# A two-layer streaming encoder step on one core: the FFN's second product as a seven-product 2x2x2 block scheme, with operand sums kept in DRAM

## The chip, the core and the metric

The kernel runs on one NeuronCore of a Trainium2 chip. Five engines work side by side, each on its own in-order instruction list: TensorE (PE; matrix products into the accumulation memory PSUM, with its weight loads shown apart as PEld), VectorE (DVE), ScalarE (ACT), GpSimd (POOL) and SyncE (SP), which here does nothing but issue transfers. Sixteen DMA engines move data between DRAM and the on-chip memory SBUF (128 partitions). The metric is the device time of one execution in microseconds (us): median 2997.3 over three runs, from 2995.75 to 2997.85.

## What is computed

One step of an encoder with two layers, on 1024 new "prompt" frames and 64 "sample" frames, handled together as 1088 tokens (`T`) of width 1024 (`D`). Layer 0 is a state-space mixer (SSD) with an FFN behind it, layer 1 a banded attention with an FFN; every part is normalised before and after. The part that matters here:

```python
def swiglu(u, w_in, w_out):
    g, up = jnp.split(u @ w_in, 2, axis=-1)
    return (jax.nn.silu(g) * up) @ w_out
...
xp = xp + rmsnorm(swiglu(rmsnorm(xp, nw[2]), ffn_w_in[layer], ffn_w_out[layer]), nw[3])
```

`w_in` is 1024 x 5632, `w_out` 2816 x 1024. The hidden matrix between the two products has 2816 rows = 22 blocks of 128 (`FT`), for 1088 tokens. The second product, hidden times `w_out`, is what is changed. Everything is float32; each operand is split into a rounded high part and a rest (`h`, `l`), and one 128 x 128 block of a product costs three matmuls: high by high, high by rest, rest by high.

## The kernel before

**Layout and order.** Activations lie transposed: features on the partitions, tokens along the columns. `SL` cuts the tokens into three slices of 384, 384 and 320 columns, `QS` into four quarters of 256, 256, 288 and 288. The order of PE is written by hand: a clock `st.t` in the source advances with each matmul put down, and side tasks (generators: norms, loads, attention steps) are resumed when their due time on that clock has come, so PE's list is fixed when the kernel is built. The other engines' lists are ordered by a scheduler with priorities (`tc.high_priority`; `HIP` is 3000, `LDP` 1500).

**Weights.** Class `Weights` loads each weight tile by SP into a `raw` buffer (two, plus up to `lent.cap` borrowed from the ring `rx`), splits it with one ACT copy and one DVE subtraction (L338, L339) into one of three `hl` buffers, and hands it to PE. `pair` (L288 to L307) forms the sums of weight blocks for the first product on POOL and DVE.

**First product of the FFN.** It already uses the seven-product scheme of 2x2x2 blocks (`run_pair`, one call per hidden block `t_`): the token halves are `b=0` (quarters 0 and 1, 256 wide) and `b=1` (quarters 2 and 3, 288 wide). Six blocks (`NB0`) are first done plainly for `b=0` (`plain_pairs`), while `b=1` is still being prepared; then 16 blocks for both halves, about 21 us each, then the six once more for `b=1` alone, about 11 us each. Each finished hidden tile goes to DRAM (`hscr`): POOL multiplies gate by value (L1293, L1297), SP writes (L1294, L1298).

**Second product.** `loader` fetches `hscr` slice by slice into staging tiles `sg`, and ACT and DVE split them into `rx` and `r` tiles (L1326 to L1328). For each slice `s`, each of 8 output blocks `m` and each of 22 hidden blocks `k`, PE does three matmuls (L1463 to L1465):

```python
PE.matmul(ps[:, :n], wh, xh, start=(k == 0), stop=False)
PE.matmul(ps[:, :n], wh, xl, start=False, stop=False)
PE.matmul(ps[:, :n], wl, xh, start=False, stop=(k == FT - 1))
```

That is 1584 matmuls in each layer. ACT copies each finished PSUM tile to `y` (L1478) and squares it, POOL adds the squares (L477). When a slice is done its `end` task runs: `rb_steps` has PE transpose the sums of squares (`nst`, L484), DVE make the inverse root in nine or ten small steps (L495 to L508), PE spread it again (`nbp`, L514); DVE then scales `y`, adds the residual and SP writes it out. In layer 0 `end` goes on to split `y` for the attention's projections (L1398, L1399), forms a second norm `rb_out` and marks the slice in `done2`. In layer 1 the last slice's `end` is the tail of the kernel: it takes the last tile's squares straight from PSUM (L1474), sums them by a matmul with ones (L489), and lets PE do part of the residual additions (L1357, L1368).

**Attention.** After layer 0, PE projects V, K and Q of the first head pair, slice after slice (L451 to L453). Each Q's low part is copied to the other partition half by a small SBUF transfer (`Ql`, L1604) before the scores (L1676, L1677) use it.

Of the kernel before, what the change touches and what calls it, by code (L numbers as in the profile page):

```python
# [16 lines left out]
P = 128  # L17
# [16 lines left out]
FT = 22  # L34
AH = 16
# [13 lines left out]
EP_W, ER_W, EQ_W = (9.4, 9.4, 2.2), (8.9, 8.9, 3.3), (11.0, 11.0)  # L49
# [4 lines left out]
LDP, ENP, ATP = 1500, (0, 0, 1500), 1000  # L54
# [18 lines left out]
MMR = 2360.0  # L73

# [148 lines left out]
class Weights:  # L223
# [118 lines left out]
    def scaled(self, it, r):  # L342

        self.used.append(self.hl)
        t = self.hl.get()
        for k in range(KD):
            sl, c = slice(k * P, (k + 1) * P), it["kscale"][:, k:k + 1]
            self.nc.scalar.activation(t[:, 0, sl], r[:, sl], AF.Copy, scale=c)
        for k in range(KD):
            sl, c = slice(k * P, (k + 1) * P), it["kscale"][:, k:k + 1]  # L350
            self.nc.vector.scalar_tensor_tensor(t[:, 1, sl], r[:, sl], c, t[:, 0, sl], op0=ALU.mult, op1=ALU.subtract)  # L351
        it["w"] = t[:, 0, :], t[:, 1, :]
# [20 lines left out]
def hybrid_kernel(  # L373
# [36 lines left out]
    hd_ = [dr.tile([P, FT, T], F32, name=f"hscr{i}") for i in range(2)]  # L410
# [32 lines left out]
    def passes(ps, w, rhs, ks, n, parts=2, first=True, last=True):  # L443
# [4 lines left out]
        for i, (kw, k) in enumerate(ks):  # L448
# [4 lines left out]
            PE.matmul(ps[:, :n], l_, xh, start=False, stop=(last and i == nk - 1))  # L453
# [11 lines left out]
    def ssum_start(n):  # L465
        t = nsb.tile([P, 384], F32, tag="ssum", bufs=3, name="ssum")
        if n % P:
            G.memset(t[:, n:], 0.0)
        return t
# [100 lines left out]
    for b in range(2):  # L570
        for half in range(2):
            W.plan(*[dict(src=[w_so[m][:, half * 1024:(half + 1) * 1024]]) for mg in MGS for m in mg])

# [61 lines left out]
    with ExitStack() as es:  # L635
# [426 lines left out]
        finish(2)  # L1062
        for grp in order:
# [147 lines left out]

    def ffn_plan(layer):
        w1, w2 = w_f1[layer], w_f2[layer]
        W.plan(*[dict(src=[w1[i]], acc=t_ < NACC) for t_ in range(NB0) for i in (t_, FT + t_)])
        for t_ in [*range(NB0, FT), *range(NB0)]:
            W.plan(dict(src=[w1[t_], w1[FT + t_]]))
        for s in range(NSL):
            for m in range(KD):
                for k0, nk in KCH:
                    W.plan(dict(src=[w2[m][:, k0 * P:(k0 + nk) * P]], n=nk * P))  # L1220

    KCH = ((0, 8), (8, 8), (16, 6))

    def plain_pairs(ts, ops, hd, px, tmp):
# [3 lines left out]
        for q in range(2):  # L1228
            st.wait_for(lambda: all(a_ in ops.plain for a_ in (f"a{q + 1}1", f"a{q + 1}2")))
            uq = ops.plain[f"a{q + 1}1"] + ops.plain[f"a{q + 1}2"]  # L1230
            for t_, w2 in zip(ts, ws):
                x = tmp.tile([P, n], F32, tag=("p1", "u3")[q] + f"{t_ % 2}", name="x")
# [5 lines left out]
                def mult(ps):  # L1238
                    with tc.high_priority(HIP):
                        V.tensor_tensor(x, ps[:, :n], x, op=ALU.mult)  # L1240
                    nc.sync.dma_start(hd[:, t_, q * n:(q + 1) * n], x)
# [744 lines left out]
```

## Time and profile before

| | |
|---|---|
| median of the runs | 2997.3 us |
| the profiled execution, its time | 2997.29 us |
| its span, first to last instruction | 2995.6 us |
| time around the span | 1.7 us |
| mean granted TensorE clock | 0.994 |
| PE matmuls | 2948.2 us busy, 98% of the span |
| DVE, ACT, POOL | 2044.8, 1460.1 and 699.0 us busy |
| SP's transfer queue | 325.45 MB, 34.3% of sixteen engines' span |

The busy time of PE is a union: matmuls overlap, each lasts about 0.3 us and a new one starts every 0.12 to 0.17 us, so a stage's length is read from the distance between starts. Columns of the stage table: length, busy time (and count) of PE, PEld, DVE, ACT and POOL, the granted clock, the DMA engines' share and rate.

### The profile page before, as it was taken

The page shows a single profiled execution, that of the slowest core. Times are in us where ns is not written, and L with a number is a line of the kernel's source. Part 1 is how long each engine was busy: PE and PEld are TensorE (multiplying, and loading weights), DVE is VectorE, ACT ScalarE, POOL GpSimd, SP SyncE. Part 2 cuts the span into 40 slices and gives each one's busy share as a digit, 9 for nine tenths or more (in the row PEclk, how much of TensorE's full clock was granted, in tenths as well). Part 3 has the DMA queues.
Part 4 walks back from the last instruction along what each step waited for, and adds up shares of the span by engine and source line. Part 5 has one row for each costly group of instructions (what it writes and reads, how often), then busy time and mean ns, then how long its engine had stood idle before and what let it go on. Part 6 is the DMA issues. An engine that isn't in the chain of part 4 may idle for free.

```text
span 2995.6 us, 56513 instructions
## 1 busy us (share of the span) xinstructions
PE 2948.2 (98%) x21722; PEld 2891.8 (97%) x21722; DVE 2044.8 (68%) x4512; ACT 1460.1 (49%) x2643; POOL 699.0 (23%) x848
## 2 busy tenths in 40 slices
PE   8999999999999999999999999999999999999999
PEld 7999999999999999999999899999899999999999
DVE  7778887885768554574557778777778655475544
ACT  6756566564453232244445566555654322244443
POOL 1333333330121433351111000000131343451111
PEclk9999999999999999999999999999999999999999
DMA  3011111124654222255655222222356222245654
GB/s 122 33 59 51 61 50 49 61 68 145 192 150 141 83 73 80 76 161 173 202 177 169 87 76 79 70 65 86 116 171 188 80 76 77 80 148 176 214 179 136
DMA packets 180671, 335.43 MB, mean 112 GB/s; under 512 B 18192, under 2 KB 128400, under 8 KB 180400
## 3 DMA queue, kind: packets, MB, share of 16 engines
q1 hardware_dynamic: 178608, 325.45, 34.3%
q0 software_dynamic: 1792, 6.36, 1.1%
q8 instruction: 171, 2.80, 0.4%
q14 instruction: 100, 0.82, 0.1%
HBM read 264.69 MB, written 62.60 MB: 109 GB/s over the span
## 4 chain that ended last, share of the span: by engine, by line
PE 88%; DVE 7%; DMA 2%; ACT 2%; issue 1%; POOL 0%; SPq 0%; DVEq 0%; ACTq 0%; POOLq 0%
PE px L1264 9%; PE px L1265 9%; PE px L1266 9%; PE mm L451 8%; PE mm L453 8%; PE mm L452 8%; PE po L1464 6%; PE po L1465 6%; PE po L1463 6%; PE mmx L452 3%; PE mmx L451 3%; PE mmx L453 3%; PE po L1747 2%; PE ptp L1708 1%; PE yp L889 1%
## 5 line engine op out<-in xcount | busy, mean ns | idle before, releaser
L451 PE MATMUL mm<-r,hl 128*128 128x384 f32 (+2 forms) x1664 | 554.3, 333 | 6.4 <-DVE dt L698 3.4
L453 PE MATMUL mm<-r,hl 128*128 128x384 f32 (+2 forms) x1664 | 539.9, 324 | 3.2 <-DVE hl L351 2.6
L452 PE MATMUL mm<-r,hl 128*128 128x384 f32 (+2 forms) x1664 | 539.0, 324 | 0.0
L339 DVE TENSOR_TENSOR hl<-raw,hl 128x1024 fp32r<-128x1024 f32 (+1 forms) x219 | 260.6, 1191 | 219.9 <-ACT hl L338 217.3
L1265 PE MATMUL px<-r,hl 128*128 128x288 f32 (+1 forms) x1184 | 348.0, 294 | 0.0
L451 PEld LDWEIGHTS mm<-r,hl 128*128 128x128 f32 x1664 | 315.9, 190 | 9.0 <-ACT BT L775 3.7
L453 PEld LDWEIGHTS mm<-r,hl 128*128 128x128 f32 x1664 | 314.8, 189 | 4.6 <-DVE hl L351 3.7
L452 PEld LDWEIGHTS mm<-r,hl 128*128 128x128 f32 x1664 | 316.1, 190 | 0.0
L1264 PE MATMUL px<-r,hl 128*128 128x288 f32 x1056 | 311.3, 295 | 0.1
L1266 PE MATMUL px<-r,hl 128*128 128x288 f32 x1056 | 311.1, 295 | 0.0
L338 ACT CAST hl<-raw 128x1024 fp32r<-128x1024 f32 (+1 forms) x219 | 219.0, 1006 | 179.9 <-PE po L1465 97.1
L477 POOL TENSOR_TENSOR ssum<-ssum,sq 128x256 f32<-128x256 f32 (+3 forms) x97 | 128.4, 1324 | 640.6 <-ACT sq L476 625.3
L1265 PEld LDWEIGHTS px<-r,hl 128*128 128x128 f32 x1184 | 222.7, 188 | 0.0
L1266 PE MATMUL px<-rx,hl 128*128 128x256 f32 x768 | 216.5, 282 | 4.9 <-DVE hl L339 4.9
L1264 PE MATMUL px<-rx,hl 128*128 128x256 f32 x768 | 217.0, 283 | 0.6 <-ACT hl L338 0.6
L1464 PE MATMUL po<-rx,hl 128*128 128x384 f32 (+1 forms) x624 | 201.7, 323 | 0.1
L1264 PEld LDWEIGHTS px<-r,hl 128*128 128x128 f32 x1056 | 198.7, 188 | 0.5 <-DVE u L1279 0.5
L1266 PEld LDWEIGHTS px<-r,hl 128*128 128x128 f32 x1056 | 198.5, 188 | 0.0
L1463 PE MATMUL po<-rx,hl 128*128 128x384 f32 (+1 forms) x608 | 197.6, 325 | 0.0
L1465 PE MATMUL po<-rx,hl 128*128 128x384 f32 (+1 forms) x608 | 196.7, 323 | 0.0
L1265 PE MATMUL px<-rx,hl 128*128 128x256 f32 x640 | 180.1, 281 | 0.0
L288 POOL TENSOR_TENSOR tt<-raw 128x512 f32<-128x512 f32 x40 | 53.7, 1343 | 439.3 <-DMA raw<-in_w_f_dram 382.8
(367 smaller groups left out, 8163.3 us busy)
## 6 DMA issues: line engine op xcount, KB each, us to landing
raw<-in_w_f_dram SPq DMA_DIRECT2D x154, 512.0 KB, 3.8
rx<-in_w_f_dram SPq DMA_DIRECT2D x54, 512.0 KB, 3.6
raw<-in_w_in_dram SPq DMA_DIRECT2D x40, 512.0 KB, 3.5
sg<-hscr SPq DMA_DIRECT2D x88, 192.0 KB, 3.6
raw<-in_w_f_dram SPq DMA_DIRECT2D x44, 384.0 KB, 3.2
raw<-in_w_so_dram SPq DMA_DIRECT2D x32, 512.0 KB, 3.7
raw<-in_w_kv_dram SPq DMA_DIRECT2D x18, 512.0 KB, 3.5
raw<-in_w_o_dram SPq DMA_DIRECT2D x16, 512.0 KB, 3.6
```

The source lines that it names most:

```text
L338: self.nc.scalar.copy(h, v)
L339: (eng or self.eng or self.nc.vector).tensor_tensor(lo, v, h, op=ALU.subtract)
L451: PE.matmul(ps[:, :n], h_, xh, start=(first and i == 0), stop=False)
L452: PE.matmul(ps[:, :n], h_, xl, start=False, stop=False)
L453: PE.matmul(ps[:, :n], l_, xh, start=False, stop=(last and i == nk - 1))
L477: (eng or G).tensor_tensor(ssum[:, :n], ssum[:, :n], q[:, :n], op=ALU.add)
L1264: PE.matmul(ps, wh, ah[:, k, :], start=(k == 0), stop=False)
L1265: PE.matmul(ps, wh, al[:, k, :], start=False, stop=False)
L1266: PE.matmul(ps, wl, ah[:, k, :], start=False, stop=(k == 3))
L1463: PE.matmul(ps[:, :n], wh, xh, start=(k == 0), stop=False)
L1464: PE.matmul(ps[:, :n], wh, xl, start=False, stop=False)
L1465: PE.matmul(ps[:, :n], wl, xh, start=False, stop=(k == FT - 1))
```

## The change

The second product becomes a 2x2x2 block product of the hidden matrix (token halves by two hidden halves of 11 blocks, `K2`) with `w_out` (two hidden halves by two output halves of 4 blocks), with seven block products in place of eight, for each `b`.

- **Weight sums.** `side_sums` builds the four sums of weight blocks in DRAM (`tscr`) by transfers alone: per layer 16 plain copies (SP) and 16 accumulating ones (POOL), each 128 rows of 1408 floats, 15 units of the source's clock apart (`TS_W`). Each is tied to the matmul last put down (`now`). Layer 0's run beside the SSD stage, layer 1's beside the attention and its output projection.
- **Hidden sums.** `Hidden.put` collects the four tiles of a hidden pair (`k`, `k + 11`, two rows), writes three of them, and has POOL form four sums in place (288 or 256 wide), each written to DRAM: seven writes per `k` and half where there were four. The order of the first product's blocks becomes 0, 11, 1, 12, ..., 7, 18 for both halves (`BOTH`), then 8, 19, 9, 20, 10, 21 for `b=1` (`PL`).
- **Products outermost.** `SEQ` runs the seven operands one after the other, each for 4 output blocks and both halves; only the last, `s4`, takes the halves one after the other. `loader` fetches two blocks per transfer, into the tile that it splits; the staging tiles are gone from here.
- **PSUM to `yq`.** ACT's copy stays for the first operand; the other six are added or subtracted by DVE into quarter-wide tiles `yq`.
- **Norms by quarter.** `end(q)` runs per quarter: quarters 1 and 2 are complete after `a22`, quarter 0 after `s4` of `b=0`, quarter 3 at the end. `u_task` then splits slices 1, 0, 2 for the attention, whose projections take slice 1 first. In the tail of layer 1 the direct squares from PSUM and the matmul with ones are gone.
- **Borrowed buffers.** `W.lent.cap` is 0 (was 2) while the last six blocks of the first product run, and 1 in the second product until `s4` of `b=1`.
- The scaled weights of the attention are split at a raised priority.

```diff
+    def side_sums(layer):
...
+        def now(x):
+            tc.add_manual_dep(x.ins, last[0].ins.name, AT, reason="its turn")
+        def plain(p, i, src):
+            now(nc.sync.dma_start(td[:, p, i], src))
+        def more(p, i, src):
+            now(G.dma_start(td[:, p, i], src, accum_op=ALU.add))
+        for p in range(4):
+            plain(p, 0, w2[p][:, :KH])
+            yield 0, TS_W
...
+    PL = [t_ for k in range(K2 - NB0 // 2, K2) for t_ in (k, k + K2)]
+    BOTH = [t_ for k in range(K2 - NB0 // 2) for t_ in (k, k + K2)]
+    SEQ = (
+        ("a11", (0, 1)), ("s2", (0, 1)), ("s3", (0, 1)), ("s1", (0, 1)), ("a22", (0, 1)), ("a12", (0, 1)),
+        ("s4", (0,)), ("s4", (1,)),
+    )
...
+            if len(got) == 4:
+                g = G.tensor_tensor
+                s3 = self.tmp.tile([P, 288], F32, tag=f"s3{b if k in BOTH else k % 2}", name="s3")[:, :self.ops[b].n]
+                g(s3, got["a11"], got["a21"], op=ALU.subtract)
+                self.write("s3", b, k, s3)
+                g(got["a21"], got["a21"], got["a22"], op=ALU.subtract)
+                self.write("s1", b, k, got["a21"])
+                g(got["a11"], got["a21"], got["a11"], op=ALU.subtract)
+                self.write("s2", b, k, got["a11"])
+                g(got["a12"], got["a12"], got["a11"], op=ALU.add)
+                self.write("s4", b, k, got["a12"])
...
-            for s, (o, n) in enumerate(SL):
-                for m in range(KD):
-                    ps = px.tile([P, 512], F32, tag="mm", name="po")
+            for op, bs in SEQ:
+                for p in range(4):
+                    ps = {b: px.tile([P, 512], F32, tag="mm", name="po")[:, :ops[b].n] for b in bs}
                     for k0, nk in KCH:
                         w = W.get()
+                        for b in bs:
+                            for k in range(k0, k0 + nk):
+                                PE.matmul(ps[b], wh, xh, start=(k == 0), stop=False)
+                                PE.matmul(ps[b], wh, xl, start=False, stop=False)
+                                PE.matmul(ps[b], wl, xh, start=False, stop=(k == K2 - 1))
...
+                            elif op == "s2":
+                                V.tensor_tensor(c12, ps[b], c11, op=ALU.add)
+                            elif op == "s1":
+                                V.tensor_tensor(c22, ps[b], c21, op=ALU.subtract)
+                                V.tensor_tensor(c12, ps[b], c12, op=ALU.subtract)
...
+                        if op in ("a22", "s4"):
+                            q = q2 if op == "a22" else q1
...
+                            for m in (4 + p, p) if op == "a22" else (p, 4 + p):
+                                add_sq(sums[q], yq[q][:, m, :], n, m == (4 if op == "a22" else 0), V if lastp and p == 3 else None)
...
-                    if m == KD - 1 and s == NSL - 1 and rb_out is None:
-                        more = ssum_start(n)
-                        A.activation(more[:, :n], ps[:, :n], AF.Square)
...
-        for s in range(2):
+        for s in (1, 0):
             st.wait_for(lambda: s in done)
```

388 lines of the change are left out of this document (239 added, 149 removed).

## The prediction

> **What bounds the kernel now.** I read the page's engine totals first, then its chain of waits.
>
> ```profile
> PE 2948.2 (98%) x21722; PEld 2891.8 (97%) x21722; DVE 2044.8 (68%) x4512; ACT 1460.1 (49%) x2643; POOL 699.0 (23%) x848
> ...
> PE 88%; DVE 7%; DMA 2%; ACT 2%; issue 1%; POOL 0%; SPq 0%; DVEq 0%; ACTq 0%; POOLq 0%
> ```
>
> PE is busy for 98% of the span, and 88% of the chain that ended last is PE itself. Next comes the table of stages, since an average says nothing of the stage that is changed. The columns are length, then PE, PEld, DVE, ACT and POOL (busy us, count), granted clock, DMA share, GB/s.
>
> ```profile
> 55.00:684.00 629.00, 618.35 (x4294) 596.59 (x4293) 512.02 (x1340) 392.64 (x623) 202.10 (x374) 0.99 0.17 56
> 1690.00:2155.00 465.00, 452.22 (x3684) 428.63 (x3683) 358.30 (x1114) 275.71 (x676) 4.72 (x27) 0.99 0.25 75
> ...
> 1290.00:1357.00 67.00, 67.00 (x505) 66.82 (x504) 54.81 (x82) 33.43 (x55) 37.28 (x28) 1.00 0.48 147
> 1359.70:1623.54 263.84, 263.72 (x1610) 263.11 (x1609) 144.33 (x219) 121.62 (x197) 37.01 (x24) 1.00 0.60 187
> 2720.70:2982.30 261.60, 261.60 (x1596) 261.50 (x1596) 122.95 (x166) 104.17 (x161) 31.32 (x24) 1.00 0.58 181
> ```
>
> The rows are SSD, attention, the last six blocks of the first product in layer 0, and the second product of each layer. The second product never lets PE stop, at full clock, with DVE at 55% or less: its length is the number of matmuls times their pitch, and what removes matmuls there removes time. The stage before it is the tightest for DVE, 54.81 of 67 us.
>
> **The pitch by width.** A matmul lasts twice its pitch, so I take first and last start of an unbroken run of one width. The four pairs lie 11, 14, 7 and 12 starts apart.
>
> ```profile
> 1365.95 0.33 PE L1463 MATMUL po<-r,hl 128*128 128x384 f32 x1
> ...
> 1367.86 0.34 PE L1465 MATMUL po<-r,hl 128*128 128x384 f32 x1
> ...
> 1569.83 0.31 PE L1464 MATMUL po<-rx,hl 128*128 128x320 f32 x1
> ...
> 1571.88 0.31 PE L1463 MATMUL po<-rx,hl 128*128 128x320 f32 x1
> ...
> 999.76 0.28 PE L1265 MATMUL px<-rx,hl 128*128 128x256 f32 x1
> ...
> 1000.58 0.28 PE L1266 MATMUL px<-rx,hl 128*128 128x256 f32 x1
> ...
> 1000.70 0.29 PE L1264 MATMUL px<-r,hl 128*128 128x288 f32 x1
> ...
> 1002.30 0.28 PE L1264 MATMUL px<-rx,hl 128*128 128x256 f32 x1
> ```
>
> This gives 1.91/11 = 0.1736 us at 384 columns, 2.05/14 = 0.1464 at 320, 0.82/7 = 0.1171 at 256 and 1.60/12 = 0.1333 at 288.
>
> **Matmuls removed.** Before, a layer has 8 x 22 x 3 = 528 matmuls for each slice: 1056 x 0.1736 + 528 x 0.1464 = 260.6 us (the stage rows say 261 to 264). After, each b has 7 x 4 x 11 x 3 = 924: 924 x 0.1171 + 924 x 0.1333 = 231.4. The difference is 29.2 us a layer, 58.4 in all. Columns times matmuls fall by an eighth; the time falls by 11.2%, as narrow matmuls cost a little more per column. The sum is made against the profiled execution: its span of 2995.6 and 1.7 around it give 2997.3, the median of the runs. Floor: 2997.3 - 58.4 = 2938.9. All that follows is charged on top.
>
> **Other engines in the second product.** Weight blocks to split fall from 3 x 8 x 22 = 528 to 32 x 11 = 352, hidden columns to split rise from 22 x 1088 = 23,936 to 77 x 544 = 41,888.
>
> ```profile
> L339 DVE TENSOR_TENSOR hl<-raw,hl 128x1024 fp32r<-128x1024 f32 x24 | 29.4, 1225 | 41.1 <-ACT hl L338 40.6 <-DMA rx<-in_w_f_dram 0.5
> ...
> L1328 DVE TENSOR_TENSOR rx<-sg,rx 128x384 fp32r<-128x384 f32 x10 | 6.0, 637 | 1.8 <-ACT rx L1327 1.7
> ```
>
> DVE saves 176 x 1225/8 = 27 us and spends 17,952 x 637/384 = 30 us; the 56 PSUM tiles a layer, with one or two additions of about 0.45 us each, add 25 to 40. That makes some 175 of 231 us, 76%: tighter, still covered by PE. Transfers: 41,888 columns x 512 bytes and 352 x 64 KB are 44.5 MB, 192 GB/s over 231 us against 187 now. So the stage stays PE's. I charge 1 us (0 to 4) for the changes of operand and for `s4`, which takes each weight chunk for one half at a time: 33 x 0.117 = 3.9 us per 11 blocks, where before 11 blocks lasted 33 x 0.1736 = 5.7.
>
> **Hidden sums.** Per pair `k` and half, four more POOL operations, 88 a layer, and 66 more writes.
>
> ```profile
> L1293 POOL TENSOR_TENSOR u<-u,c 128x288 f32<-128x288 f32 x44 | 63.6, 1446 | 67.4 <-ACT u L1292 67.4
> ...
> L1297 POOL TENSOR_TENSOR c<-p,u 128x288 f32<-128x288 f32 x44 | 40.3, 917 | 0.4
> ...
> 1086.89 0.81 POOL L1297 TENSOR_TENSOR c<-p,u 128x288 f32<-128x288 f32 x1
> 1098.97 1.31 POOL L288 TENSOR_TENSOR tt<-raw 128x512 f32<-128x512 f32 x1 [11.28 <-DMA raw<-in_w_f_dram]
> ...
> 1312.63 1.81 POOL L1297 TENSOR_TENSOR c<-p,u 128x288 f32<-128x288 f32 x1
> 1314.38 1.32 POOL L288 TENSOR_TENSOR tt<-raw 128x512 f32<-128x512 f32 x1
> ```
>
> With both halves (16 blocks), POOL idles 10 to 11 us in each block of 21; eight sums at 0.9 to 1.4 us fall on every second block and fit the gap: nothing. In the last six blocks there is no gap: the weight sum `tt` starts as the hidden tile ends. There three or four sums of 1.2 to 1.45 us stand ahead of the next `tt`, some 4.3 us late, three times a layer, while `lent.cap` 0 leaves only the two `raw` buffers as stock. If all were lost it is 6 x 4.3 = 26 us. Behind a late `tt` stand its DVE sums, its split, and then PE. For it speaks that the splits of slice 0, which ran there, shrink (quarters of 256 instead of a slice of 384, first needed for one operand of 11 blocks). I charge 3.5 us, bounds 0 to 26, nearer the lower end since PE has no idle time in that stage now and a weight tile has two more split behind it in `hl`.
>
> **Weight sums through DRAM.** Thirty-two transfers of 704 KB a layer, none like them in the trace. Nearest rows:
>
> ```profile
> raw<-in_w_f_dram SPq DMA_DIRECT2D x154, 512.0 KB, 3.8
> ...
> hl<-in_w_f_dram POOLq DMA_DIRECT2D x7, 512.0 KB, 9.7
> ...
> DMA to landing us min/median/max: 1.9/2.1/4.3
> ```
>
> By size, my estimate is 3.8 x 704/512 = 5.2 us for a plain copy and 9.7 x 704/512 = 13.3 for an accumulating one, every 15 us, in the stages with the lowest DMA shares of the table (0.17 and 0.25). POOL's issues cost 16 x 0.9 us a layer; what queues behind one that waits for its matmul is POOL work of the SSD stage, busy 202 of 629 us. What can be hurt is a small transfer on the attention's path: the third row is the landing of `Ql`, 48 of them, 1.9 to 4.3 us, and no wait for it is among PE's waits in that stage. A `Ql` that follows a plain copy lands at 2.1 + 5.2 = 7.3 us, 3.0 beyond what is known to be covered; 48 issues in 477 us meet a copy's 5.2 us about every second time, so 16 copies give 8 x 3.0 = 24 us if no further cover exists. I charge 2 us (0 to 24), as heads are interleaved and PE has other matmuls at hand. [...]
>
> **Norms by quarter.** Four in place of three chains, and in layer 0 both norms: three more chains, with six extra PE transposes, 0.2 each, 1.2 us. At the seam to the attention the first thing left over is quarter 0's chain, between slice 1's and slice 0's projections:
>
> ```profile
> 1627.73 0.49 PE L484 MATMUL nst<-ident,ssum 128*128 128x128 f32 x3
> ...
> 1628.41 0.55 DVE L495 TENSOR_REDUCE nv<-nst 128x3 f32<-128x384 f32 x1
> ...
> 1630.38 0.16 DVE L508 SCALAR_TENSOR_TENSOR nr<-nv 128x3 f32<-128x3 f32 x1
> ```
>
> From `nst` to `nr` takes 2.8 us; before, PE had a dozen matmuls in between. In the new order only six (1.04 us) stand between `nst` and `nbp`, so PE waits about 2; another chain may do the same. I charge 2.5 (0 to 6).
>
> **The tail.**
>
> ```profile
> 2982.63 0.44 ACT L1474 ACTIVATE ssum<-po 128x320 f32<-128x320 f32 x1 [8.14 <-PE po L1465]
> ...
> 2983.99 0.16 DVE L498 TENSOR_SCALAR nv<-nst 128x3 f32<-128x3 f32 x1 [0.40 <-PE nst L489]
> ...
> 2987.05 3.79 DVE L1366 SCALAR_TENSOR_TENSOR y<-y,pcs,rb 128x320 f32<-128x320 f32 x8 [1.32 <-ACT rb L517]
> ```
>
> Now 1.4 us pass from the last square's start to the norm's first step. After, an addition (0.45), the square (0.44), its sum (0.5), transposes (0.5) and a reduction (0.55) make some 2.5 to 2.8; the eight scalings at 288 columns give 0.4 back. Charge 1.0 (0 to 2).
>
> **Sum.** 2938.9 + 1 + 3.5 + 2 + 1.2 + 2.5 + 1.0 = 2950.1, so 2950.
>
> **Rivals.**
>
> A. *POOL and DVE become the bound in the last six blocks.* Twelve more sums of 1.3 us make POOL's 37.28 into 53 of 67 us, and if POOL and DVE hold each other up, a good part of it falls on DVE's chain. For it: the same multiplication takes 1446 ns on one line and 917 on the other, as if it waited for something. Against it: 54.81 + 37.28 = 92 us already fit into 67. If 10 to 13 us a layer come through, the time is 2950 - 3.5 + 24 = 2971 (2962 to 2985). [...]
>
> B. *Slower: the hidden tiles have one buffer each.* DVE's product for the next pair writes a tile only after the sums made in place there have reached DRAM. Place: each change of pair in the 16-block loop, 16 in both layers. Available are about 10.5 us from one pair's last tile to the next use; the chain is 0.45 + 0.81 + three sums of 1.45 and a landing:
>
> ```profile
> hscr<-c SPq DMA_DIRECT2D x44, 144.0 KB, 3.5
> ...
> DMA to landing us min/median/max: 1.7/3.0/8.9
> ```
>
> With 3.5 us it is 9.1 and fits; with the largest, 8.9, it is 14.5, 4.0 late, 16 x 4.0 = 64 us: 2950 + 64 = 3014, and with two thirds of it about no change. It decides from 48/16 = 3 us per change on. The median lands well short of that.
>
> C. *The pace does not come.* If 256 columns go no faster than 288 here, 924 x 0.0162 x 2 = 30 us are lost: 2980. The run quoted above speaks against it.
>
> **How the numbers follow.** Forecast (2938 to 2962) 0.60, A 0.21, C 0.04, B 0.15, a quarter of it within 0.2% (6 us, about what a measurement of this kernel can tell from no change), the rest slower. The range takes the forecast's lower end, the floor, and reaches over most of A: 2938 to 2982, with about 0.2 outside. Faster 0.85, same 0.04, slower 0.11.
>
> **What will show it.** Second product: 231 to 235 us a layer, PE without waits; last six blocks: 66 to 70 us, or 77 and more with PE waiting for `hl` (A); the 16-block loop: 338 us as before, or waits of PE for px with DVE waiting on an `hscr` write (B); attention: no PE wait on `Ql`; seam: one stall of 1 to 4 us on `nbp`. What would make it wrong is a stage other than these that grows: a copy delaying the SSD stage's POOL list, or the larger DVE load in `s4`.

## The result

The changed kernel takes 3031.6 us (median of 4 runs, 3029.47 to 3032.71) against 2996.5 us before (2994.49 to 2997.85): a ratio of 1.0117, 95% interval 1.0099 to 1.0134. It is slower by 35 us where 47 us of gain were forecast, and it lies outside the predicted range.

The page after the change, the same two lines as before the change: busy time of the engines, and the shares of the chain of waits.

```profile
PE 2916.3 (96%) x22247; PEld 2850.9 (94%) x22247; DVE 2104.0 (69%) x4679; ACT 1447.8 (48%) x2677; POOL 903.7 (30%) x1081
...
PE 30%; DVE 6%; DMA 3%; ACT 2%; issue 2%; POOL 1%; SPq 0%; POOLq 0%; DVEq 0%; ACTq 0%
```

PE has 32 us less busy time, as intended, but it is busy for 96% of a longer span. The second line cannot be set beside the 88% of before: its shares add up to 44%, as the chain could be followed back to 1687 us only; PE is 30 of these 44. The list of what PE waited for (PE's line, the engine's line that it waited for, us in total, times, longest one) shows the new stalls; these are the main rows that are new or have grown.

```profile
PE po L1572 <- DVE hl L342: 16.7, 6, 4.2
PE px L1356 <- DVE u L1371: 13.3, 6, 4.3
PE px L1356 <- DVE p L1373: 7.1, 4, 2.7
PE S L1815 <- DVE pT L1852: 6.7, 13, 2.0
PE px L1358 <- DVE hl L342: 6.7, 3, 3.1
...
PE mm L458 <- DVE hl L355: 4.2, 3, 2.2
...
PE nbp L519 <- DVE nr L513: 3.8, 3, 3.0
PE nst L489 <- DVE nv L512: 3.7, 1, 3.7
```

All rows of that list add up to 106 us, against 42 us before the change. Next the table of stages (length, busy PE, PEld, DVE, ACT, POOL, granted clock, DMA share, GB/s): the last six blocks and the second product of layer 0, the stretch from there to the first value product of the attention, 140 us in the midst of the second product, then the two stages again in layer 1.

```profile
1302.70:1388.20 85.50, 74.66 (x517) 73.17 (x517) 57.01 (x76) 32.08 (x51) 56.20 (x44) 0.94 0.41 132
1388.20:1635.70 247.50, 236.78 (x1874) 235.48 (x1874) 162.64 (x286) 111.93 (x204) 41.66 (x39) 0.98 0.60 193
1635.70:1711.40 75.70, 65.69 (x363) 62.67 (x362) 64.84 (x201) 44.64 (x130) 11.69 (x14) 0.91 0.33 107
1420.00:1560.00 140.00, 140.00 (x1138) 140.00 (x1137) 75.94 (x123) 59.64 (x101) 10.42 (x13) 1.00 0.61 197
2690.40:2774.10 83.70, 74.03 (x517) 72.86 (x516) 57.28 (x76) 30.43 (x49) 56.39 (x44) 0.94 0.41 133
2774.10:3014.10 240.00, 233.03 (x1864) 232.44 (x1862) 147.89 (x249) 100.68 (x174) 29.68 (x33) 0.99 0.61 195
```

The same stretch to the first value product before the change:

```profile
1623.60:1686.90 63.30, 60.94 (x374) 59.24 (x372) 54.08 (x163) 37.04 (x96) 1.75 (x7) 1.00 0.37 113
```

Two things stand in these rows. Where the second product is left alone, PE never stops and the clock is 1.00; at its edges PE falls short of the length, and the granted clock drops to 0.91 to 0.98. The mean clock over the span is 0.9848 after and 0.9945 before. That is 3027.8 x 0.0152 = 46 us of clock not granted, against 2995.6 x 0.0055 = 16.5 before.

The stages, cut at the first and last start of the matmuls of the two FFN products, sum to the difference of the spans:

| stage | before, us | changed, us | difference |
|---|---|---|---|
| up to the first FFN block of layer 0 (SSD and projections) | 951.6 | 961.2 | +9.6 |
| first product, plain pairs and 16 blocks, layers 0 and 1 | 339.4 + 338.8 | 341.5 + 340.9 | +4.2 |
| first product, last six blocks | 68.7 + 68.8 | 85.5 + 83.7 | +31.7 |
| second product | 263.9 + 262.0 | 247.5 + 240.0 | -38.4 |
| between the FFNs (attention) | 689.3 | 713.8 | +24.5 |
| tail | 13.1 | 13.7 | +0.6 |
| span | 2995.6 | 3027.8 | +32.2 |

By cause the same 32 us are: 58.4 of matmuls saved, 64 more of PE's waits, 30 more of clock not granted. That makes 35; of the clock not granted, 4 us more than before fall into waits of PE, where they cost nothing.

The pitch that the saving rests on, from the middle of the changed second product (start, duration, line; the three rows lie 15 starts apart):

```profile
1440.48 0.28 PE L1570 MATMUL po<-rx,hl 128*128 128x256 f32 x1
...
1442.19 0.29 PE L1570 MATMUL po<-r,hl 128*128 128x288 f32 x1
...
1444.19 0.28 PE L1570 MATMUL po<-rx,hl 128*128 128x256 f32 x1
```

They give 1.71/15 = 0.114 us at 256 columns and 2.00/15 = 0.133 at 288.

### The profile page after: what moved, and what is told of

It is laid out like the page before. It is cut to its first block, busy times and chain, and to the rows that moved or that the text cites. A ratio compares the mean times of both kernels' runs of the same rounds, so it can differ in the third digit from the quotient of the medians.

```text
span 3027.8 us, 58411 instructions
## 1 busy us (share of the span) xinstructions
PE 2916.3 (96%) x22247; PEld 2850.9 (94%) x22247; DVE 2104.0 (69%) x4679; ACT 1447.8 (48%) x2677; POOL 903.7 (30%) x1081
## 3 DMA queue, kind: packets, MB, share of 16 engines
q8 instruction: 175, 2.87, 0.4%
## 5 line engine op out<-in xcount | busy, mean ns | idle before, releaser
L342 DVE TENSOR_TENSOR hl<-raw,hl 128x1024 fp32r<-128x1024 f32 (+2 forms) x219 | 250.4, 1144 | 155.3 <-ACT hl L341 154.6
L1356 PE MATMUL px<-r,hl 128*128 128x288 f32 x1056 | 314.2, 298 | 13.5 <-DVE u L1371 13.3
L341 ACT CAST hl<-raw 128x1024 fp32r<-128x1024 f32 (+2 forms) x219 | 204.2, 938 | 201.1 <-PE po L1572 95.6
L482 POOL TENSOR_TENSOR ssum<-ssum,sq 128x256 f32<-128x256 f32 (+1 forms) x108 | 113.7, 1059 | 532.8 <-ACT sq L481 520.2
L1572 PE MATMUL po<-r,hl 128*128 128x288 f32 x616 | 182.8, 297 | 4.0 <-DVE hl L342 4.0
L1572 PE MATMUL po<-rx,hl 128*128 128x256 f32 x616 | 173.0, 281 | 12.7 <-DVE hl L342 12.7
L1570 PE MATMUL po<-r,hl 128*128 128x288 f32 x616 | 183.2, 297 | 0.0
L1571 PE MATMUL po<-r,hl 128*128 128x288 f32 x616 | 182.8, 297 | 0.0
```

Of the source, the lines that this page charges most:

```text
L341: self.nc.scalar.copy(h, v)
L342: (eng or self.eng or self.nc.vector).tensor_tensor(lo, v, h, op=ALU.subtract)
L482: (eng or G).tensor_tensor(ssum[:, :n], ssum[:, :n], q[:, :n], op=ALU.add)
L1356: PE.matmul(ps, wh, ah[:, k, :], start=(k == 0), stop=False)
L1570: PE.matmul(ps[b], wh, xh, start=(k == 0), stop=False)
L1571: PE.matmul(ps[b], wh, xl, start=False, stop=False)
```

## The experiments

All are edits of the changed kernel unless said otherwise. Stage lengths are read as in the table above.

**The weight sums' transfers.** e1 leaves the 64 transfers out and reads plain blocks of `w_out` instead.

```diff
-        st.spawn(side_sums(0), 100.0)
+        ts_done.append(0)
...
-            s1=lambda p: td[:, p, 0], s3=lambda p: td[:, p, 1], s2=lambda p: td[:, p, 2], a22=lambda p: td[:, p, 3],
+            s1=lambda p: w2[p][:, h1], s3=lambda p: w2[p + 4][:, h2], s2=lambda p: w2[p + 4][:, h1], a22=lambda p: w2[p][:, h2],
```

> The 64 transfers that form the weight sums in DRAM are left out, and the second product reads plain blocks of w_out in their place (its values are other ones, its work is the same). Theory A, the copies delay small transfers of the SSD stage's end and of the attention: the first FFN block starts at about 952 us as before the change (961 in the changed kernel), the 3.7 us wait of PE for a norm near 690 us goes, with two or three clock windows of 3.4 us at half speed, and the attention shrinks by some 6 to 9 us; in all 14 to 20 us less, about 3013 to 3017. Rival, the SSD stage is longer by chance of instruction order and the attention by its norms: under 5 us less.

It took 3015.5 us, 16 less, as theory A had it. The SSD stage ends at 952.1, and the stretch between the FFNs is 5.2 us shorter (theory A had 6 to 9). The timeline of the changed kernel near the SSD stage's end (start, duration, engine, line; in brackets the idle time before it and what ended it) shows how:

```profile
678.14 0.82 POOL L591 DMA_DIRECT2D tscr<-in_w_f_dram  x1
...
679.60 9.39 SPq L633 DMA_DIRECT2D yt<-yscr  x4
...
687.68 0.48 DVE L634 SCALAR_TENSOR_TENSOR yt<-yt,pcs,rb 128x256 f32<-128x256 f32 x1 [3.17 <-DMA yt<-yscr]
...
691.49 0.88 PE L489 MATMUL nst<-ident,ssg 128*128 128x128 f32 x3 [3.67 <-DVE nv L512]
```

POOL issues a weight-sum transfer at 678.14. The first of SP's four loads of `yt`, issued at 679.60 on SP's own queue, lands after 8.1 us (3.7 in the kernel before), and the four take 9.39 us to go out one after the other; DVE waits 3.17 us for one, its norm is late, and PE stands 3.67 us on that norm. The same places without the transfers:

```profile
676.72 5.22 SPq L633 DMA_DIRECT2D yt<-yscr  x4
...
684.98 0.53 PE L489 MATMUL nst<-ident,ssg 128*128 128x128 f32 x3 [1.80 <-DVE ssg L961]
```

Four loads in 5.22 us and a wait of 1.80. In the attention the time from issue to landing of `Ql` (minimum, median, maximum) is, in the changed kernel and then without the transfers:

```profile
DMA to landing us min/median/max: 2.0/2.1/6.7
```

```profile
DMA to landing us min/median/max: 1.9/2.1/3.8
```

So the longest grew, to 6.7 us. It does not stand behind a transfer that SP issued, as the prediction had it, but right behind one of POOL's:

```profile
2108.84 0.81 POOL L591 DMA_DIRECT2D tscr<-in_w_f_dram  x1 [15.72 <-PE mm L458]
...
2109.41 1.94 SPq L1742 DMA_DIRECT2D Ql<-Ql  x2
```

The longest behind one of SP's own (issued at 2022.93) took 5.0 us. The attention from its first to its last value product lasts 466.0 us before, 474.8 after and 469.2 without the transfers; PE's waits in it add up to 17 us with them and 13 without. That it is `Ql` that PE waits for there is not shown, as none of PE's waits names it.

e8 only spaces the transfers 13.5 units apart in place of 15, so that they end earlier.

> The transfers of the weight sums are 13.5 units of the clock apart in place of 15, so that layer 0's are done some 48 us earlier, before the SSD stage's last norms. Theory A: the first FFN block starts at 952 to 954 us (961 in the changed kernel) and the time falls by 7 to 9 us; the attention is about as long as in the changed kernel. Rival: the copies delay the SSD stage all along it, and the start stays at 958 us or later.

It took 3023.7 us, 8 less: the first FFN block starts at 955.3 (952 to 954 expected) and the attention is as long as before that edit (474.5). One profile says little here: in the eleven kernels with 15 units the block starts between 956.0 and 961.2, though nothing in that stage differs, and in the four below with 12 units (e12, e15 to e17) between 949.6 and 953.1. So transfers that end earlier help by some 3 to 12 us, and the collision in SSD is one of place, at the stage's end.

**The last six blocks.** Four runs took one thing each.

```diff
 # e2, also in e6, e9, e12, e16 to e18
-                        W.lent.cap = 0
+                        W.lent.cap = 2
 # e3: the four sums' writes, the first of them
-                self.write("s3", b, k, s3)
+                self.write("s3", b, k, s3, nc.gpsimd)
 # e4
+                if k not in BOTH:
+                    self.write("s3", b, k, got["a11"])
...
+                    return
 # e5: in Hidden.put, for the pairs k = 7 to 9 of b = 1
+                    st.spawn(self.sums(b, k, got, 3.0), 3.0)
```

> The weights may borrow two ring buffers while the last six blocks of the first product run, as before the change. Theory B, those blocks are slow because each has only two raw buffers and its loads start late: the stage from the end of the 16 blocks to the first matmul of the second product falls from 85.6 and 84.0 us to about 70, and the time by 25 to 30 us, to about 3003. Rival C, POOL's four sums for a pair are what comes late: no change in that stage, or under 5 us in each layer. Also possible: the hidden loader now lacks the two buffers and the start of the second product waits longer, by 3 to 6 us.

> The four writes of hidden sums are issued by POOL, right behind the sums, and not by SP. Theory D, SP stands on a write that waits for a sum while weight loads queue behind it (4.7 us of SP in one such group): the stage of the last six blocks shortens by 5 to 12 us in each layer and the wait of 3.9 us at the start of the second product goes. Rival: POOL's issues at 0.8 to 0.9 us each make POOL's weight sums later still, and the stage gets longer by 3 us or more.

> In the last six blocks of the first product POOL's sums of hidden tiles are left out, and the four writes take tiles as they are (other values, the same transfers). Rival C (POOL's sums, 12 of 0.8 to 1.7 us in each layer): the stage falls to about 70 us. Theory B (two raw buffers): it stays above 78 us, since the load of a block still cannot start before a buffer of the block before is free. Theory D predicts most of the fall as well, since SP waits no longer for the sums.

> Nothing is left out. The hidden sums of the last pair of the 16 blocks (for b=1) and of the first two pairs of the last six blocks are put down one at a time, 3 units of the source's clock apart, in place of four in a row, so that neither POOL's weight sums nor SP's weight loads stand behind all of them. Theory C/D (the sums in a row, on POOL and in SP's list): the stage of the last six blocks falls from 85 to 72 to 78 us, near the 75 of the run that leaves the sums out. Theory B alone (two raw buffers): no change, 82 us or more.

> The sums put down later and two buffers lent as well. If the two causes add up, the stage of the last six blocks comes to 69 to 73 us as before the change and the waits at the start of the second product shrink: about 3000 us. If the lent buffers only move the wait to the hidden loader, it is no better than the sums put down later alone.

| run | last six blocks, layer 0 / 1, us | whole time, us |
|---|---|---|
| before | 68.7 / 68.8 | 2996.5 |
| changed | 85.5 / 83.7 | 3031.6 |
| e2, two buffers lent | 81.7 / 81.8 | 3024.2 |
| e3, sums written by POOL's queue | 81.4 / 80.6 | 3024.3 |
| e4, no hidden sums here | 75.8 / 74.6 | 3006.1 |
| e5, sums later in the source | 86.0 / 84.6 | 3029.5 |
| e6, e5 and two lent | 82.8 / 82.3 | 3023.1 |

None of the theories took the 16 us alone: e2 was to bring the stage to about 70 us, e3 to shorten it by 5 to 12, and e4's 75 lies between theory C (70) and theory B (above 78). The sums are the largest part, 9 to 10 us a layer in this stage and 25 us of the whole time. e5 did not test what it meant to: the scheduler put the three sums of a pair on POOL one behind the other all the same (1345.34, 1347.10 and 1347.99 us), and the stage did not move. The changed kernel's timeline shows one turn of the chain; rows of SP, POOL, DVE and PE follow one another.

```profile
1310.71 1.35 SPq L1422 DMA_DIRECT2D rx<-hscr  x3
...
1314.28 1.18 POOL L1313 TENSOR_TENSOR hid<-hid 128x256 f32<-128x256 f32 x1
...
1315.48 2.48 SPq L1292 DMA_DIRECT2D hscr<-hid  x5
1318.05 0.38 SPq L253 DMA_DIRECT2D raw<-in_w_f_dram  x1
...
1319.66 0.38 SPq L253 DMA_DIRECT2D raw<-in_w_f_dram  x1
...
1325.39 1.32 POOL L291 TENSOR_TENSOR tt<-raw 128x512 f32<-128x512 f32 x1 [7.77 <-DMA raw<-in_w_f_dram]
...
1326.74 1.29 DVE L309 TENSOR_TENSOR tt<-tt,raw 128x512 f32<-128x512 f32 x1 [3.95 <-POOL tt L291]
...
1329.62 0.45 DVE L1371 TENSOR_TENSOR u<-px,p 128x288 f32<-128x288 f32 x1
...
1330.12 0.40 PE L1356 MATMUL px<-r,hl 128*128 128x288 f32 x1 [2.28 <-DVE u L1371]
```

From 1312.06 to 1315.48 SP issues nothing: the next hidden write in its list waits for POOL's sum, which ends at 1315.46. Five hidden writes take 2.48 us more, the last of them again waiting for a sum; only then go the weight loads, three in 2 us. The third, issued at 1319.66, has landed 5.6 us later, when POOL's weight sum `tt`, after 7.77 us of waiting for it, starts at 1325.39; DVE's next sum of the weights waits 3.95 us for that, `u` (DVE's reading of a PSUM tile) stands behind it in DVE's list, and PE waits 2.28 us for the tile. The group of that `tt` over the stage (count, busy us, mean ns, idle time before it and what ended it):

```profile
L291 POOL TENSOR_TENSOR tt<-raw 128x512 f32<-128x512 f32 x5 | 7.1, 1414 | 32.1 <-DMA raw<-in_w_f_dram 20.3 <-DVE u L1381 11.8
```

Of 32.1 us of POOL's idle time 20.3 end with a raw weight that lands; before the change none of its idle time in this stage did. So POOL has time to spare and is not the bound. What the sums cost cannot be read from this wait, though: in e4, without them, it is 19.8 us, and the stage is 10 us shorter all the same. That they cost it through SP's list is what the rows above show for one turn; e3, which takes their writes out of that list and burdens POOL with the issues, gave back 3 to 4 us.

e9 leaves the sums out and lends two buffers.

> POOL's hidden sums are left out from the last pair of the 16 blocks (its half b=1) to the end of the first product (other values, the same writes), and two buffers are lent. If sums and missing buffers together are all that makes the last six blocks longer, that stage is back at 68 to 71 us in both layers (85.5 and 83.7 in the changed kernel, 75.8 and 74.6 without the sums alone, 81.7 with two buffers alone). If it stays at 74 or more, a third thing is at work, such as the hidden loader's transfers.

It came to 80.2 / 77.0 and 3016.1 us, longer than without the sums alone, so a third thing is at work. In its timeline (SP, ACT, PE):

```profile
1319.54 0.32 SPq L1428 DMA_DIRECT2D rx<-hscr  x1
...
1322.37 0.62 ACT L1429 CAST rx<-rx 128x512 fp32r<-128x512 f32 x1 [6.33 <-DMA rx<-hscr]
1322.90 1.04 ACT L341 CAST hl<-raw 128x1024 fp32r<-128x1024 f32 x1
...
1323.99 0.40 PE L1362 MATMUL px<-r,hl 128*128 128x288 f32 x1 [2.46 <-ACT hl L341]
```

SP issues a hidden load at 1319.54. ACT stands 6.33 us on the split of a hidden tile, and the cast of a weight, `hl`, which PE needs, is behind it in ACT's list. Before the change such loads went into staging tiles ahead of their use; now a load may start only when the tile that it is split in is free, so the split in the list meets a transfer that is still under way.

e13 puts the splits later, tied to a matmul; e12 ties the sums to matmuls (what e5 meant), lends two buffers and issues layer 0's weight sums every 12 units; e15 is splits later, sums tied and the 12 units; e16 all four.

```diff
 # e13, also e15, e16 (e17, e18: 5.0, and only in the last six blocks)
-                                A.copy(h, f)
-                                V.tensor_tensor(l_, f, h, op=ALU.subtract)
+                                    x = A.copy(h, f)
+                                    tc.add_manual_dep(x.ins, last[0].ins.name, AT, reason="its turn")
+                                    V.tensor_tensor(l_, f, h, op=ALU.subtract)
...
+                            st.spawn(split(), 7.0)
 # e12, also e15 to e18
+            def g(*a, **kw):
+                x = G.tensor_tensor(*a, **kw)
+                if d:
+                    tc.add_manual_dep(x.ins, last[0].ins.name, AT, reason="its turn")
...
+                    st.spawn(self.sums(b, k, got, 4.0), 4.0)
```

> Correct values. The sums of the last pair of the 16 blocks (b=1) and of the next two pairs are each tied to a matmul 4, 8, 12 and 16 units of the clock behind the pair, so that POOL cannot run them in a row; two buffers are lent; layer 0's weight sums are issued every 12 units. If theories A to D hold: SSD back at 952 to 955, the last six blocks at 70 to 76, the second product's start with a shorter wait, in all 2996 to 3006 us. If POOL in its order of work is the bound by itself, the last six blocks stay at 80.

> Nothing is left out. The hidden loader issues its transfers as before, but the ACT copy and the DVE subtraction of a loaded tile are put down 7 units of the clock later, tied to a matmul, so that they no longer stand in ACT's and DVE's lists in front of weight casts while the transfer is under way. Theory H (ACT held at its head by a hidden load): ACT's waits of 3 to 7 us for a hidden transfer go, the last six blocks fall from 85 to 74 to 80 us, and the 4 to 6 us wait at the start of the second product shrinks to under 2 us. Rival (sums and buffers alone): no more than 2 us gained in either place, or a longer start, since the hidden tiles are ready later.

> Correct values. Hidden splits later, sums tied to matmuls 4 units apart, layer 0's weight sums every 12 units; no buffers lent. If all three are causes and add up: last six blocks 70 to 74 us, SSD 953, in all 2996 to 3004 us. If the sums and the splits are the same wait seen twice, 77 or more.

> As the run before, with two buffers lent as well. If the third raw buffer pair matters once the lists are free: 69 to 71 us in the last six blocks, as before the change, and the start of the second product without a wait over 2 us; 2990 to 3000 us in all. If lending only takes buffers from the hidden loader, it is 2 to 5 us slower than the run without.

| run | last six blocks | second product | sum of the four | whole time, us |
|---|---|---|---|---|
| before | 68.7 / 68.8 | 263.9 / 262.0 | 663.4 | 2996.5 |
| changed | 85.5 / 83.7 | 247.5 / 240.0 | 656.7 | 3031.6 |
| e2, two lent | 81.7 / 81.8 | 244.8 / 236.9 | 645.2 | 3024.2 |
| e4, no hidden sums | 75.8 / 74.6 | 248.7 / 240.4 | 639.5 | 3006.1 |
| e12, sums tied, two lent | 78.1 / 78.0 | 249.5 / 239.2 | 644.8 | 3010.3 |
| e13, splits later | 81.3 / 82.1 | 255.0 / 245.8 | 664.2 | 3035.0 |
| e15, splits later, sums tied | 81.3 / 81.5 | 252.5 / 244.8 | 660.1 | 3022.2 |
| e16, splits later, sums tied, two lent | 72.9 / 72.7 | 252.4 / 246.2 | 644.2 | 3007.7 |

In the last six blocks two buffers or later splits alone are worth 2 to 4 us a layer, tied sums with two buffers 6 to 7, all three 11 to 13 of the 15 to 17 lost. But PE has only moved its wait behind the stage's end: by the sum of both stages (which scatters by 2 to 3 us among kernels that change nothing there) two lent buffers gain 11 us, tied sums and later splits add nothing to that, and without lent buffers later splits lose. What e12 and e16 are faster than e2 by lies outside these stages, about half of it in the SSD stage with its transfers 12 units apart. So buffers and sums are shown to cost time; that the lists of ACT and DVE cost some of it on top is argued from the rows of e9, and no run has clearly gained by freeing them.

**Versions.** e17 keeps the splits later only while the last six blocks run; e18 also runs both layers' weight sums beside the SSD stage, 7 units apart.

```diff
+    def both_sums():
+        yield from side_sums(0)
+        yield from side_sums(1)
...
-        st.spawn(side_sums(0), 100.0)
+        st.spawn(both_sums(), 100.0)
```

> As e16 (sums tied, two buffers lent, layer 0's weight sums every 12 units), but the hidden splits are put down later, by 5 units, only while the last six blocks run, and at once in the second product. If the longer start of the second product in e16 (252.4 and 246.2 us against 247.5 and 240.0) comes from the later splits, those two stages fall by 4 to 8 us each while the last six blocks stay at 72 to 75: 2996 to 3002 us. If the start waits for the weights anyway, no change: 3005 to 3009.

> As e17, and the weight sums of both layers run beside the SSD stage, 64 transfers 7 units apart, none beside the attention. Theory A: the attention from first to last value product falls from 475 to 469 us, as without copies in e1, and the SSD stage stays at 950 to 955 if the transfers end before its last norms: 4 to 6 us less than e17. Rival: at twice the rate they slow the SSD stage's small transfers all along, and it grows by more than 5 us.

e17: 3010.8 us (ratio 1.0041, 1.0026 to 1.0055); the second product stays at 254.5 / 244.0, so it is not the splits put later within it that make it long. Those put later before it do: PE's wait at its start is 3.89 us in e12 and 11.03 in e17, which differ in them alone.

```profile
1380.65 0.58 PE L1587 MATMUL po<-rx,hl 128*128 128x256 f32 x1 [3.89 <-DVE hl L342]
```

```profile
1386.45 0.58 PE L1599 MATMUL po<-rx,hl 128*128 128x256 f32 x1 [11.03 <-DVE hl L342]
```

e18: 3003.2 us (ratio 1.0020, 1.0010 to 1.0029). Its attention from first to last value product is 469.0 us, as without the transfers, and SSD ends at 954.6. It is the fastest version of the change and still slower than the kernel before. What holds its second product at the start (ACT, then PE):

```profile
1373.84 0.68 ACT L1445 CAST r<-r 128x576 fp32r<-128x576 f32 x1 [4.35 <-DMA r<-hscr]
1374.42 0.62 ACT L1445 CAST rx<-rx 128x512 fp32r<-128x512 f32 x1
...
1387.55 0.58 PE L1603 MATMUL po<-rx,hl 128*128 128x256 f32 x1 [10.74 <-DVE hl L342]
```

ACT stands 4.35 us on a hidden load, more splits of hidden tiles follow it, and PE waits 10.74 us for a weight. These are the splits that were put later in the last six blocks. That a better order of loads there would remove the wait was not tried.

**From the second product to the first score.** This stretch is 36.7 us before and 48.9 after. The two rows are PE's transposes of one norm's squares and its spread:

```profile
1659.16 0.38 PE L489 MATMUL nst<-ident,ssum 128*128 128x128 f32 x2
...
1663.58 0.66 PE L519 MATMUL nbp<-ident,nr 128*128 128x128 f32 x2 [2.97 <-DVE nr L513]
```

PE stands 2.97 us on the spread of quarter 0's norm. e10 leaves out four residual additions on DVE, e7 gives the residual additions to POOL, e14 puts the spread later.

```diff
 # e7
-                eng = V
+                eng = G
 # e10
+                        if layer or q in (1, 2):
+                            eng.tensor_tensor(yh[h], yh[h], xr[h], op=ALU.add)
 # e14
-EP_W, ER_W, EQ_W = (4.0, 7.0, 7.0, 5.0), (5.0, 8.9, 8.9, 7.0), 24.0
+EP_W, ER_W, EQ_W = (4.0, 7.0, 7.0, 5.0), (9.0, 8.9, 8.9, 9.0), 24.0
```

> In the quarter ends of the second product POOL adds the residual, not DVE: two additions of 4 blocks for each quarter. Theory E, between the second product and the attention DVE is the bound (95% busy there, two quarters' ends and two slices' splits instead of one of each): the time from the last matmul of the second product to the first score, 46 to 49 us (36.7 before the change), falls by 3 to 8 us. Rival F, it is the order of the norm's steps (PE stands 3.0 us on one spread of a norm): that stretch stays within 2 us, and POOL, slower at an addition, may make it longer.

> In layer 0 the residual additions of quarters 0 and 3 are left out (four additions of 1.2 to 1.35 us on DVE, other values): about 5 us less DVE work in the stretch where DVE is 90% busy. Theory E (DVE is the bound from `s4` to the first score): PE gains 4 to 8 us between the second product's end part and the first score (last s4 wait, seam to first score 46 to 49 us). Theory F (order of the norms): the 3 us wait on the spread of a norm and the stretch stay within 2 us.

> The second half of a norm of quarters 0 and 3 (PE's spread) is due 9 units of the clock behind its first half, in place of 5 and 7. Theory F: the 3.0 us wait of PE on that spread goes, with one or two half-clock windows: the stretch to the first score 44 us or less (48.9 in the changed kernel). Rival: the wait only moves to the product that needs the norm, and the stretch is within 2 us of before; the tail may get longer by 1 us.

The stretch was 52.9 us in e7 (3054.1 in all, with a second product of 256.8 / 250.3), 51.8 in e10 (3031.6) and 50.1 in e14 (3031.3, the wait on the spread now 3.7 us). In the eight kernels that change nothing there (e1 to e6, e8, e9) it is 45.9 to 47.8, so some 9 to 12 us are lost in it. Neither less work on DVE nor another due time shortens it. Which of its waits comes first stays open.

**What a stall costs.** e11 is the kernel before with 12 stalls put into its second products.

```diff
+    def stall(k):
+        sp = ax("nst")
+        for i in range(3):
+            PE.transpose(sp[:, i * P:(i + 1) * P], ident, ident)
...
+            V.tensor_reduce(a, sp[:, :3 * P].rearrange("p (a b) -> p a b", b=P), axis=mybir.AxisListType.X, op=ALU.add)
+            V.tensor_tensor(h, a, a, op=ALU.mult)
+            for _ in range(k):
+                V.tensor_tensor(h, h, a, op=ALU.mult)
+            V.tensor_tensor(r[:, :3], h, a, op=ALU.mult)
+        bp = ax("nbp")
+        for i in range(3):
+            PE.transpose(bp[:, i * P:(i + 1) * P], r[:, i:i + 1].to_broadcast([P, P]), ident)
```

> The kernel before, with 12 extra stalls put into its second products, where PE else never waits: PE transposes a constant, DVE runs a chain of small steps on it, PE transposes the result. The chains have 1, 4, 8 (layer 0, two each) and 12, 16, 24 steps (layer 1), so that PE stands for about 1.2 to 6 us; the stalls are some 30 us apart. Theory G, a stall costs its length and, from some length on, one or two windows of 3.4 us at half clock (1.7 us of work each): short ones cost only themselves, those of 3 us and more 1.7 to 3.4 us on top; about 40 us of waits and 15 to 25 us of clock in all. Rival: the clock windows in the changed kernel have another cause, and none stand at these stalls.

Three of the stalls on PE's timeline, then the 15 us around each in the table of stages (the granted clock is the third figure from the right):

```profile
1390.02 0.51 PE L525 MATMUL nbp<-ident,sr 128*128 128x128 f32 x3 [2.92 <-DVE sr L522]
...
1429.92 0.51 PE L525 MATMUL nbp<-ident,sr 128*128 128x128 f32 x3 [2.92 <-DVE sr L522]
...
1494.86 0.87 PE L525 MATMUL nbp<-ident,sr 128*128 128x128 f32 x3 [5.81 <-DVE sr L522]
```

```profile
1385.00:1400.00 15.00, 12.07 (x64) 11.83 (x63) 4.90 (x7) 2.68 (x4) 1.34 (x1) 0.89 0.36 101
1425.00:1440.00 15.00, 12.08 (x72) 11.84 (x71) 4.83 (x8) 3.73 (x5) 1.27 (x1) 1.00 0.34 97
1488.00:1503.00 15.00, 9.19 (x43) 8.95 (x42) 13.54 (x32) 7.61 (x13) 1.34 (x1) 0.77 0.51 167
```

A wait of 2.92 us is followed once by a clock of 0.89 over 15 us, which is one window of 3.41 us at half clock, and once by none; one of 5.81 us by two windows (0.77). In layer 0 the six waits add up to 23.7 us and the second product grew by 39.5 (263.9 to 303.4); in layer 1 by 58.7 for 41.3. So these stalls, of 2.9 to 10.7 us, cost on average 2.6 to 2.9 us each beyond themselves, the six inserted transposes among it. Theory G holds in kind: half-clock windows stand at eleven of the twelve stalls. In size it was too small: 65 us of waits where about 40 were expected, and about 30 us more of clock not granted than before the edit (3104.0 x 0.015 = 46.6 against 16.5), the worth of some 18 windows, where 15 to 25 us were. The shortest stall came to 2.92 us, so that shorter ones cost only themselves was not tested. The records of the changed kernel have 27 full half-clock windows of 3.41 us, those of the kernel before 9.

## Why the prediction was wrong

**Matmuls removed: right.** The pitch came out at 0.114 and 0.133 us (0.1171 and 0.1333 forecast), PE is without a gap in the midst of the second product, and rival C falls. The floor of 2938.9 is real; 93 us were charged on top of it where the forecast had 11.

**Every charge: sized as the wait alone.** The step "From `nst` to `nr` takes 2.8 us ... so PE waits about 2" and its like count a stall at its length. What the runs showed is a second price: the 18 more half-clock windows are worth 30 us, nearly half of what the waits themselves cost. This could have been read before: the rows of SSD and attention before the change have a clock of 0.99, the second product's 1.00. The windows last 3.41 us each in the records, and waits of 2.04, 2.28 and 2.57 us were already followed by one in the last six blocks.

**"Hidden sums": the step that failed most.** It charged 3.5 us, "nearer the lower end since PE has no idle time in that stage now"; the stage grew by 31.7, of which e4 gives back 18.8 when the sums are left out. PE, busy for 67.00 of 67 us, had no idle time to take up a delay with, so that reason spoke for a higher charge. And POOL's "there is no gap" was read from one moment: it was busy for 37.28 of 67 us there before. Rival A named the place and nearly the size (10 to 13 us a layer, 15 to 17 measured), but not the mechanism: POOL does not become the bound, it idles 20.3 us for weights in the stage. That POOL and DVE hold each other up, as the rival supposed, was not shown by any run; that idle time speaks against it as the cause. What the runs show in its place are lists in order: SP's, with weight loads behind hidden writes that wait for sums (e4), and only two raw buffers, which take away the stock that hid it (e2). That ACT's and DVE's lists, with weight casts behind splits of hidden tiles still in transfer, are a third part is seen in the rows of e9, but no run clearly gained by freeing them over both stages. That part had no price at all in the prediction, though the change says that the staging tiles are gone. The 13 us of the stage's growth that are not the sums are not split further.

**"Weight sums through DRAM": right in kind, too small, and the wrong place first.** 2 us were charged, on the attention alone; e1 showed 16 us, 9.1 of them in the two profiles at the end of the SSD stage, where the small loads of `yt` land late beside a transfer of POOL's. For the attention the upper bound of 24 was far off (5 to 6 us measured). That bound added a copy's own landing time of 5.2 us to the 2.1 of a `Ql` behind it, an estimate of the author's that no run shows: the copies landed in 4.3 to 4.5 us (medians), the longest `Ql` behind one took 5.0 us in place of 7.3, and the two slowest transfers shown, 6.7 us for `Ql` and 8.1 for `yt`, stand beside one that POOL issued.

**Second product's edges and the seam: too small.** 1 us for changes of operand and 2.5 for the seam stand against 20 us of saving lost in the second products and 12 us on the way to the first score. At the start of each second product PE waits 3.9 to 4.2 us for a weight. In layer 0 it waits 3.45 us more at the second of `s4`'s output blocks, while DVE has no time to spare (columns as in the table of stages):

```profile
1585.00:1601.00 16.00, 11.37 (x93) 10.97 (x91) 15.97 (x20) 8.93 (x24) 9.02 (x8) 1.00 0.81 271
```

```profile
1600.98 0.46 PE L1572 MATMUL po<-rx,hl 128*128 128x256 f32 x1 [3.45 <-DVE hl L342]
```

DVE is busy for 15.97 of 16 us with the end of quarter 2 and the attention's splits, both of which follow `a22`, and the split of the weight comes among them; before the change PE had no such wait in the second product. The prediction named a larger DVE load in `s4` as what might make it wrong. Its estimate of DVE's load, 76%, was on the safe side as a mean (162.64 of 247.50 us is 66%), but a mean says nothing of the edges. What the 12 us of the seam wait for stays open.

**Rival B falls.** The 16-block loops grew by about 2 us a layer, not by 32.

**The tail** lost 0.6 us where 1.0 was charged.

## What to carry to other kernels

A kernel whose PE is 98% busy has no slack to lose: before a change of operands is priced by matmuls, follow every load that it adds or moves through the list of the engine that issues it and of the engine that first touches it, and ask what stands behind it (here three weight loads, the first issued at 1318.05, behind hidden writes for which SP had stood from 1312.06 to 1315.48 us). Price a stall at its length plus the clock lost behind it, so that ten waits of 3 us cost nearer 45 us than 30: an estimate, from the probe's three stalls of 2.9 to 3.5 us, two of which brought a window of 3.41 us at half clock, 1.7 us lost each. When a repair shortens one stage, add up the next one too: here several only moved the wait. Long background transfers belong where no small transfer is waited for; moving them away from the end of a stage gave back 8 us for a one-line edit.

## What was not expected of the hardware

Half-clock windows came after PE waits of 2.04 us (in the last six blocks of layer 1), 2.28 (in the rows shown above) and 1.93 (in the attention of the kernel before), and in lengths of 3.41 or 6.83 us; a wait of 2.87 us in the last six blocks of layer 1 brought none, and the same wait of 2.92 us cost a window once and none once. A transfer of 704 KB that accumulates landed in 7.0 us (median of 32), about half the 13.3 estimated from POOL's smaller ones. The changes in the last six blocks did not add: 4 us for two buffers and 10 for no sums made 5 to 7 together.
